# mLSTM heads: row statistics spread by two products with ones instead of small products and diagonals

## The chip, the cores and the metric

The kernel runs on one core of a Trainium2 chip. Its time is the device time of one execution, in microseconds (us); three executions were timed. One further execution was recorded by the profiler, and all rows of the trace come from that one. The engines are PE (TensorE, products; PEld is its weight load), DVE (VectorE), ACT (ScalarE), POOL (GpSimd) and SP (SyncE, which here only issues transfers).

## The reference

The network has two layers on 512 rows of width 1024. The first layer's mixer joins four heads of an mLSTM (192 channels each) and four heads of attention over a memory of 256 rows; an output projection and a gated convolutional MLP follow, then a second layer with banded attention. The part that the change touches is the end of an mLSTM head:

```python
den = jnp.sum(s, axis=-1) + inter * jnp.einsum('bhtd,bhd->bht', qq, n_st)
h = num / jnp.maximum(jnp.abs(den), jnp.exp(-m_t))[..., None]
...
hm = hm * lax.rsqrt(jnp.mean(hm * hm, axis=-1, keepdims=True) + EPS)
hm = hm.reshape(bsz, seq, A_WIDTH) * a_head_g[a].astype(jnp.float32)
mix_out = (hm * jax.nn.sigmoid(o.astype(jnp.float32))).astype(x.dtype)
```

The division by the denominator and the normalisation behind it can be taken together: num times the inverse root of mean(num²) + EPS * max(den², exp(-2 m)). Both kernels do it in this form. `m` is the running stabiliser of a row, and the term with it is called the floor here.

## The kernel before

Activations lie with channels on the 128 partitions and the 512 rows along the free axis. A product in full precision is three products of rounded halves (`mm3`, L166 to L168): high by high, high by low, low by high. The halves come from `split`: a cast on ACT (L122) gives the high half, a subtraction on DVE (L123) the low one. Weights arrive in a raw buffer `wr` by SP's queue and are split in the same way into `wh` and `wl`, of which there are three each; other pools are `u` (57 tiles of 128x512), `t` (8), `bias` (4), and the PSUM banks `mm` (3, in rows `pmm`), `sc` (3, `psc`) and `tr` (2, `ptr`).

`gate_rows` computes the gates once, ahead of the heads. Four rows of 512 (one a head) hold the gates' cumulative sums (`br`), `ar` and the stabiliser (`mr`). The mask exponents go to DRAM (`rowd`) and come back spread over all partitions; `ar` and `mr` are turned to columns by eight 4x4 transposes (L1056, L1057), and ACT makes `floor2` = exp(-2 m) from the second.

`mlstm_head(h)` is a generator. It makes four tiles of weighted scores (L1136: exponential of the mask row; L1142: times the scores, then a split into `pt`), and multiplies them with the values into two `tr` banks: one holds 128 channels, the other 64 channels and, on the other 64 partitions, the denominator 64 times over. ACT squares both banks (L1171) into `t`; DVE multiplies the numerators with the output gate `og` (L1173), which frees the banks. Then, per head:

- eight small products (L1180, L1181; 128x2 out) with the table `mcf` sum the squares of each row over the channels and pick its denominator, with rows now on partitions;
- DVE forms max(den², floor) * EPS + mean (L1185 to L1187, 128x4 each), its inverse root by an integer guess and three Newton steps (`rsqrt`, L214 to L220), and two diagonal tiles of it (`diagonal`, L122, L123 in small, then L229);
- two products of ones with these diagonals (`spread`, L242) bring the factor to all partitions, where it multiplies `og` in place (L1194); each result is split into a pair of tiles in `mixes`, the out-projection's operands.

While a head runs, `weave` advances a second generator, the fill, by so many steps for each yield of the head: projections (`project`, one step is one `mm3`) during heads 0 to 2, pieces of the output projection (`outp.part`) during head 3. The memory attention runs between heads 1 and 2 and between heads 2 and 3. In the profile head 0 ends at about 132 us, head 1 at 163, head 2 at 218, head 3 at 256; its `mixes` are the last operands that the out-projection needs. Where a step needs a tile of these, the code writes out the yields; the order on each engine is then fixed by a scheduler at build time, from the program's dependences, except for operations inside `pin`, which keep their place in program order. Each engine works through its own list in order.

Of the kernel before, what the change touches and what calls it, by code (L numbers as in the profile page):

```python
# [16 lines left out]
P = 128  # L17
# [34 lines left out]
def trunk(  # L52
# [34 lines left out]
    def ps(tag):  # L87
        count[0] += 1
        return psum.tile([P, S], F32, tag=tag, name=f"p{tag}{count[0]}", bufs=pbufs[tag])

    def small(n=4):
        return sb("s", [P, 32])[:, :n]
# [15 lines left out]
    mcf = cpool.tile([P, 3, 2], F32, name="mcf")  # L108
    V.memset(mcf, 0.0)
    V.memset(mcf[:, 0, 0:1], 1.0)  # L110
    V.memset(mcf[:HD, 1, 0:1], 1.0)
    V.memset(mcf[HD:, 1, 1:2], 1.0 / HD)
    V.memset(mcf[:HD, 2, 1:2], 1.0 / HD)
    V.memset(mcf[HD:, 2, 0:1], 1.0)


# [121 lines left out]
    def spread(dgs, tag):  # L238

        o = ps(tag)  # L240
        for i, dg in enumerate(dgs):
            nc.tensor.matmul(o, onesr, dg, start=i == 0, stop=i == 1)  # L242
        return o
# [76 lines left out]
    G.dma_start(gateb, bass.AP(tensor=a_gate_b.tensor, offset=a_gate_b.offset, ap=[[0, P], [1, 2 * AH]]))  # L320
# [39 lines left out]
    def keep(l, i, os_):  # L360
        t = sb("u", [P, S])
        for c, o in enumerate(os_):
            V.tensor_copy(t[:, c * MEM : (c + 1) * MEM], o)
        G.dma_start(spill[l][:, i * S : (i + 1) * S], t)
# [113 lines left out]
    keep(1, 1, vo)  # L478

# [508 lines left out]
    floor2 = cpool.tile([P, TT, AH], F32, name="floor2")  # L988
    RO = [0, 512, 896, 1152, 1280]

    rowd = dram.tile([TT, AH, S], F32, name="rowd")

    def gate_rows():
# [58 lines left out]
        V.tensor_scalar(mr, mr, -40.0, None, op0=ALU.max)  # L1052
        yield
        tp = ps("tr")
        for T in range(TT):
            nc.tensor.transpose(tp[:, T * AH : (T + 1) * AH], ar[:, T * P : (T + 1) * P], ident[:AH, :AH])  # L1056
            nc.tensor.transpose(tp[:, 16 + T * AH : 16 + (T + 1) * AH], mr[:, T * P : (T + 1) * P], ident[:AH, :AH])  # L1057
        pin(V.tensor_copy(acol, tp[:, :16].rearrange("p (t h) -> p t h", t=TT)))
        A.activation(floor2, tp[:, 16:32].rearrange("p (t h) -> p t h", t=TT), AF.Exp, scale=-2.0)
# [53 lines left out]

    def masked(h, s):

        r = exps[h, s]
        pin(
            G.affine_select(
                out=r[:, :P], in_=r[:, :P], pattern=[[1, P]], base=0, channel_multiplier=-1,
                compare_op=ALU.is_ge, fill=NEG,  # L1120
            )
        )

    def mlstm_head(h):
# [3 lines left out]
        rs = slice(HD, P) if odd else slice(0, HD)  # L1128
# [33 lines left out]
        yield from weighted_scores(3)  # L1162
        for s in range(TT if h < AH - 1 else 0):
            exponents(h + 1, s)
# [9 lines left out]
        yield  # L1174
        for s in range(TT if h < AH - 1 else 0):
            masked(h + 1, s)
        st = ps("sc")
        for T in range(TT):
            sl = slice(T * P, (T + 1) * P)
            nc.tensor.matmul(st[:, 2 * T : 2 * T + 2], sqs[0][:, sl], mcf[:, 0, :], start=True, stop=False)  # L1180
            nc.tensor.matmul(st[:, 2 * T : 2 * T + 2], sqs[1][:, sl], mcf[:, 1 + odd, :], start=False, stop=True)  # L1181
            yield 0.581
        st = st[:, : 2 * TT].rearrange("p (t c) -> p t c", c=2)
        z, fc = small(), small()
        V.tensor_tensor(out=z, in0=st[:, :, 1], in1=floor2[:, :, h], op=ALU.max)  # L1185
        V.tensor_scalar(z, z, EPS, 1e-35, op0=ALU.mult, op1=ALU.max)
        V.scalar_tensor_tensor(z, st[:, :, 0], 1.0 / DH, z, op0=ALU.mult, op1=ALU.add)  # L1187
        rsqrt(fc, z)
        dg = diagonal(fc)
        yield 2.673  # L1190
        fb = spread(dg, "sc")
        yield
# [315 lines left out]
```

## Time and profile before

| | us |
|---|---|
| median of 3 runs | 1209.37 |
| lowest and highest | 1208.14, 1210.49 |
| the profiled execution | 1208.28 |
| its span, first to last instruction | 1206.5 |
| granted clock of PE, mean | 0.999 |

A row of the timeline gives the start, the duration, the engine, the line, the operation, output and inputs, the size and how many such rows stand together; brackets give how long the engine had been idle and whose work ended that. Durations of products are modelled and overlap; the distance between two starts is what a product takes. A row of the waits view gives the engine and line that waited, whom for, and the total, the count and the longest.

### The profile page before, as it was taken

Reading aid. Unit: us, or ns where it says so; the run is one execution under the profiler, and the core shown is the slowest. Engines: PE = TensorE matmul, PEld = TensorE weight load, DVE = VectorE, ACT = ScalarE, POOL = GpSimd, SP = SyncE. Lnnn points to the kernel's source line nnn. Section 1 sums busy time; section 2 is a strip of 40 time slices with the busy share of each in tenths; the row PEclk is TensorE's granted clock in tenths of the full one; section 3 lists DMA queues with packets and bytes.
Section 4 is the critical chain, followed back from the end, with each engine's and each line's share of the span. In section 5 each row is a group of like instructions: output and inputs, shape, how many; then the busy total and the mean of one; then the engine's idle time right before and its main releaser. Section 6 shows DMA issues by size and latency. Waiting matters only on the chain.

```text
span 1206.5 us, 18758 instructions
## 1 busy us (share of the span) xinstructions
PE 1191.2 (99%) x7031; PEld 1055.1 (87%) x7031; DVE 938.8 (78%) x1719; ACT 711.9 (59%) x1253; POOL 139.5 (12%) x229
## 2 busy tenths in 40 slices
PE   8999999999999999999999999999999999999997
PEld 8898888888889999999888888888889999999986
DVE  6877688887978777777698888997896777777755
ACT  4547577654655555555565667775565555555545
POOL 0211101011011111111021000101101010111100
PEclk9999999999999999999999999999999999999999
DMA  8646413347565766665564313244845456666551
GB/s 277 200 112 144 91 54 79 109 147 193 123 151 141 161 159 147 153 145 130 148 193 129 93 53 101 68 132 153 194 101 135 114 131 140 141 140 135 121 156 70
DMA packets 206284, 161.79 MB, mean 134 GB/s; under 512 B 8328, under 2 KB 185966, under 8 KB 206194
## 3 DMA queue, kind: packets, MB, share of 16 engines
q1 hardware_dynamic: 184338, 120.78, 34.2%
q0 software_dynamic: 21856, 39.82, 17.7%
q8 instruction: 55, 0.90, 0.3%
q14 instruction: 35, 0.29, 0.1%
HBM read 132.04 MB, written 32.46 MB: 136 GB/s over the span
## 4 chain that ended last, share of the span: by engine, by line
PE 94%; ACT 3%; DVE 2%; DMA 0%; issue 0%; SPq 0%; DVEq 0%; ACTq 0%
PE pmm L166 18%; PE pmm L168 18%; PE pmm L167 18%; PE ptr L166 6%; PE ptr L167 6%; PE ptr L168 6%; PE psc L168 5%; PE psc L167 5%; PE psc L166 5%; PE psc L505 2%; PE ptr L1335 1%; ACT wh L122 1%; PE ptr L1356 1%; PE ptr L1357 1%; DMA u<-in_mem_dram 0%; PE ptr L574 0%
## 5 line engine op out<-in xcount | busy, mean ns | idle before, releaser
L166 PE MATMUL pmm<-u,wh 128*128 128x512 f32 (+1 forms) x968 | 336.6, 348 | 0.1
L168 PE MATMUL pmm<-u,wl 128*128 128x512 f32 (+1 forms) x968 | 333.5, 345 | 0.0
L167 PE MATMUL pmm<-u,wh 128*128 128x512 f32 (+1 forms) x968 | 333.2, 344 | 0.1
L123 DVE TENSOR_TENSOR wl<-wr,wh 128x1024 fp32r<-128x1024 f32 (+4 forms) x168 | 194.5, 1159 | 94.0 <-ACT wh L122 93.4
L122 ACT CAST wh<-wr 128x1024 fp32r<-128x1024 f32 (+4 forms) x168 | 167.7, 1000 | 96.1 <-PE pmm L167 42.1
L168 PEld LDWEIGHTS pmm<-u,wl 128*128 128x128 f32 x968 | 183.6, 190 | 21.1
L167 PEld LDWEIGHTS pmm<-u,wh 128*128 128x128 f32 x968 | 183.9, 190 | 18.4 <-DVE u L123 0.8
L166 PEld LDWEIGHTS pmm<-u,wh 128*128 128x128 f32 x968 | 183.7, 190 | 18.0 <-ACT u L122 0.5
L166 PE MATMUL ptr<-u,wh 128*128 128x512 f32 x272 | 106.7, 392 | 0.0
L167 PE MATMUL ptr<-u,wh 128*128 128x512 f32 x272 | 106.5, 392 | 0.0
L168 PE MATMUL ptr<-u,wl 128*128 128x512 f32 x272 | 105.8, 389 | 0.0
L736 POOL DMA_DIRECT2D xspill<-t x64 | 55.9, 873 | 411.6 <-ACT t L735 411.6
L166 PE MATMUL pmm<-u,u 128*128 128x256 f32 x296 | 84.5, 285 | 2.5 <-ACT t L812 2.5
L168 PE MATMUL pmm<-u,u 128*128 128x256 f32 x296 | 83.9, 284 | 0.2 <-DVE u L123 0.2
L167 PE MATMUL pmm<-u,u 128*128 128x256 f32 x296 | 83.8, 283 | 0.0
L123 DVE TENSOR_TENSOR u<-pt,u 128x512 fp32r<-128x512 f32 x102 | 69.9, 688 | 9.7 <-ACT u L122 7.1
L166 PE MATMUL psc<-u,wh 128*128 128x256 f32 (+1 forms) x232 | 76.1, 328 | 0.0
L735 ACT COPY t<-ptr 128x512 f32<-128x512 f32 x64 | 37.5, 585 | 65.4 <-PE ptr L168 65.4
L167 PE MATMUL psc<-u,wh 128*128 128x256 f32 (+1 forms) x232 | 75.9, 327 | 0.0
L123 DVE TENSOR_TENSOR u<-t,u 128x512 fp32r<-128x512 f32 x78 | 53.4, 689 | 22.0 <-ACT u L122 21.3
L122 ACT CAST u<-pt 128x512 fp32r<-128x512 f32 x102 | 63.0, 617 | 11.5 <-DVE pt L847 11.3
L909 ACT ACTIVATE t<-t 128x512 f32<-128x512 f32 x34 | 21.6, 634 | 80.3 <-DVE t L645 80.3
(282 smaller groups left out, 2562.5 us busy)
## 6 DMA issues: line engine op xcount, KB each, us to landing
wr<-in_ffn_w_up_dram SPq DMA_DIRECT2D x54, 512.0 KB, 4.9
wr<-in_ffn_w_down_dram SPq DMA_DIRECT2D x38, 512.0 KB, 3.8
pt<-in_ffn_w_up_dram SPq DMA_DIRECT2D x34, 512.0 KB, 6.7
xspill<-t POOLq DMA_DIRECT2D x64, 256.0 KB, 4.8
wr<-in_a_w_in_dram SPq DMA_DIRECT2D x20, 512.0 KB, 4.0
xspill<-u POOLq DMA_DIRECT2D x32, 256.0 KB, 2.9
u<-xspill SPq DMA_DIRECT2D x32, 256.0 KB, 5.2
wr<-in_w_kv_dram SPq DMA_DIRECT2D x12, 512.0 KB, 4.2
```

Source lines behind the costliest of these rows:

```text
L122: high = A.copy(hi, src) if on_act else V.tensor_copy(hi, src)
L123: low = V.tensor_tensor(out=lo, in0=src, in1=f(hi), op=ALU.subtract)
L166: nc.tensor.matmul(o, lh, rh, start=first, stop=False, skip_group_check=more)
L167: nc.tensor.matmul(o, lh, rl, start=False, stop=False, skip_group_check=more)
L168: nc.tensor.matmul(o, ll, rh, start=False, stop=last, skip_group_check=more)
L505: nc.tensor.matmul(o, a, b, start=first and i == 0, stop=i == 1)
L735: A.copy(t, o)
L736: G.dma_start(xspill[j], t, accum_op=ALU.add)
L909: A.activation(self.acc, self.acc, AF.Silu)
L1335: nc.tensor.transpose(tp[:, b * P : (b + 1) * P], es[T, h][:, b * P : (b + 1) * P], ident)
L1356: nc.tensor.matmul(o2[:, s * P :], w, hi_at(pts[h], s, s, TT - s), start=s == 0, stop=False)
L1357: nc.tensor.matmul(o2[:, s * P :], w, lo_at(pts[h], s, s, TT - s), start=False, stop=s == TT - 1)
```

## The change

It sums squares and floor on all partitions at once, and computes the inverse root there:

- the table `mcf` and its six memsets, the four transposes of `mr` and `floor2` go;
- `gate_rows` makes the floor as a row: exponential on ACT, times EPS * DH / HD with a lower limit on DVE, stored to DRAM (`floord`) from POOL's queue;
- `den_floor(h)` fetches a head's row, spread over 128 partitions, into a `bias` buffer; its place on POOL's queue is behind the fourth weighted scores and ahead of the next head's four mask rows;
- behind the squares, DVE takes the larger of the scaled den² and the floor on the 64 denominator rows (L1177), adds the two tiles (L1178), and the sum is split;
- two products with ones (L1186) sum over the partitions, the result standing on all of them; ACT takes the inverse root from the bank (L1188, with a table load of its own), DVE does one Newton step on the full tile (L1189 to L1191) and multiplies `og` as before (L1194, now from `t` and not from the bank);
- the yields of a head keep about the same sum, in two pieces instead of six;
- the transfer of the gate biases (4 KB, used first in the value projection's L976) moves from the start to behind the memory keys and values, and two transfers are pinned.

```diff
--- before.py
+++ after.py
@@ -105,15 +105,6 @@
         out=maskf, in_=maskf, pattern=[[1, P]], base=0, channel_multiplier=-1,
         compare_op=ALU.is_ge, fill=NEG,
     )
-    mcf = cpool.tile([P, 3, 2], F32, name="mcf")
-    V.memset(mcf, 0.0)
-    V.memset(mcf[:, 0, 0:1], 1.0)
-    V.memset(mcf[:HD, 1, 0:1], 1.0)
-    V.memset(mcf[HD:, 1, 1:2], 1.0 / HD)
-    V.memset(mcf[:HD, 2, 1:2], 1.0 / HD)
-    V.memset(mcf[HD:, 2, 0:1], 1.0)
-
-
     HEADS = (slice(0, HD), slice(HD, P))
 
     pin = tc.keep_in_program_order
@@ -317,7 +308,6 @@
                 c += k
 
     gateb = cpool.tile([P, 2 * AH], F32, name="gateb")
-    G.dma_start(gateb, bass.AP(tensor=a_gate_b.tensor, offset=a_gate_b.offset, ap=[[0, P], [1, 2 * AH]]))
 
 
 
@@ -361,7 +351,7 @@
         t = sb("u", [P, S])
         for c, o in enumerate(os_):
             V.tensor_copy(t[:, c * MEM : (c + 1) * MEM], o)
-        G.dma_start(spill[l][:, i * S : (i + 1) * S], t)
+        pin(G.dma_start(spill[l][:, i * S : (i + 1) * S], t))
 
     def two_banks(*tags):
         return [ps(tag)[:, :MEM] for tag in tags]
@@ -476,6 +466,7 @@
             x_low(j - 1)
         value_products(vo, *vws1[1], 4)
     keep(1, 1, vo)
+    pin(G.dma_start(gateb, bass.AP(tensor=a_gate_b.tensor, offset=a_gate_b.offset, ap=[[0, P], [1, 2 * AH]])))
 
 
 
@@ -985,10 +976,10 @@
     e, u, c, r = (cpool.tile([P, TT, AH], F32, name=f"gate{i}") for i in range(4))
     tot = cpool.tile([AH, 16], F32, name="tot")
     acol = cpool.tile([P, TT, AH], F32, name="acol")
-    floor2 = cpool.tile([P, TT, AH], F32, name="floor2")
     RO = [0, 512, 896, 1152, 1280]
 
     rowd = dram.tile([TT, AH, S], F32, name="rowd")
+    floord = dram.tile([AH, S], F32, name="floord")
 
     def gate_rows():
 
@@ -1050,13 +1041,14 @@
             yield
         pin(V.tensor_tensor(out=mr, in0=mr, in1=br, op=ALU.add))
         V.tensor_scalar(mr, mr, -40.0, None, op0=ALU.max)
+        A.activation(mr, mr, AF.Exp, scale=-2.0)
+        V.tensor_scalar(mr, mr, EPS * DH / HD, 1e-26 * DH / HD, op0=ALU.mult, op1=ALU.max)
+        pin(G.dma_start(floord, mr))
         yield
         tp = ps("tr")
         for T in range(TT):
             nc.tensor.transpose(tp[:, T * AH : (T + 1) * AH], ar[:, T * P : (T + 1) * P], ident[:AH, :AH])
-            nc.tensor.transpose(tp[:, 16 + T * AH : 16 + (T + 1) * AH], mr[:, T * P : (T + 1) * P], ident[:AH, :AH])
         pin(V.tensor_copy(acol, tp[:, :16].rearrange("p (t h) -> p t h", t=TT)))
-        A.activation(floor2, tp[:, 16:32].rearrange("p (t h) -> p t h", t=TT), AF.Exp, scale=-2.0)
 
     mixes = [None] * KT
 
@@ -1111,6 +1103,14 @@
         pin(G.dma_start(r[:, :n], src))
         exps[h, s] = r
 
+    floors = {}
+
+    def den_floor(h):
+
+        floors[h] = sb("bias", [P, S])
+        src = bass.AP(tensor=floord.tensor, offset=floord.offset + h * S, ap=[[0, P], [1, S]])
+        pin(G.dma_start(floors[h], src))
+
     def masked(h, s):
 
         r = exps[h, s]
@@ -1125,7 +1125,7 @@
         hp, odd = divmod(h, 2)
         sh = 3 * hp + 1
         full = 3 * hp + 2 * odd
-        rs = slice(HD, P) if odd else slice(0, HD)
+        rs, ds = HEADS[odd], HEADS[1 - odd]
         pt = sb("pt", [P, 5 * S], F32R)
 
         def weighted_scores(s):
@@ -1160,6 +1160,7 @@
         yield from weighted_scores(2)
         yield from products(0)
         yield from weighted_scores(3)
+        den_floor(h)
         for s in range(TT if h < AH - 1 else 0):
             exponents(h + 1, s)
         yield from products(1)
@@ -1172,24 +1173,23 @@
             sqs.append(sq)
             V.tensor_tensor(out=og[j][r, :], in0=o[r, :], in1=og[j][r, :], op=ALU.mult)
         yield
+        sq, den = sqs
+        V.scalar_tensor_tensor(den[ds, :], den[ds, :], EPS * DH / HD, floors.pop(h)[ds, :], op0=ALU.mult, op1=ALU.max)
+        V.tensor_add(sq, sq, den)
+        hi, lo = sb("t", [P, S], F32R), sb("t", [P, S], F32R)
+        split(hi, lo, sq)
         for s in range(TT if h < AH - 1 else 0):
             masked(h + 1, s)
-        st = ps("sc")
-        for T in range(TT):
-            sl = slice(T * P, (T + 1) * P)
-            nc.tensor.matmul(st[:, 2 * T : 2 * T + 2], sqs[0][:, sl], mcf[:, 0, :], start=True, stop=False)
-            nc.tensor.matmul(st[:, 2 * T : 2 * T + 2], sqs[1][:, sl], mcf[:, 1 + odd, :], start=False, stop=True)
-            yield 0.581
-        st = st[:, : 2 * TT].rearrange("p (t c) -> p t c", c=2)
-        z, fc = small(), small()
-        V.tensor_tensor(out=z, in0=st[:, :, 1], in1=floor2[:, :, h], op=ALU.max)
-        V.tensor_scalar(z, z, EPS, 1e-35, op0=ALU.mult, op1=ALU.max)
-        V.scalar_tensor_tensor(z, st[:, :, 0], 1.0 / DH, z, op0=ALU.mult, op1=ALU.add)
-        rsqrt(fc, z)
-        dg = diagonal(fc)
-        yield 2.673
-        fb = spread(dg, "sc")
-        yield
+        yield 2.6
+        o = ps("sc")
+        for i, part in enumerate((hi, lo)):
+            nc.tensor.matmul(o, onesr, part, start=i == 0, stop=i == 1)
+        fb, t = sb("t", [P, S]), sb("t", [P, S])
+        A.activation(fb, o, AF.Abs_reciprocal_sqrt, scale=1.0 / DH)
+        V.tensor_mul(t, fb, fb)
+        V.scalar_tensor_tensor(t, t, -0.5 / DH, o, op0=ALU.mult, op1=ALU.mult)
+        V.scalar_tensor_tensor(fb, t, 1.5, fb, op0=ALU.add, op1=ALU.mult)
+        yield 3.4
         for j, r in ((full, slice(0, P)), (sh, rs)):
             V.tensor_tensor(out=og[j][r, :], in0=fb[r, :], in1=og[j][r, :], op=ALU.mult)
             if mixes[j] is None:
```

The lines of the changed kernel move: L122 and L123 are L113 and L114, L166 to L168 are L157 to L159, L1071 is L1063, L1171 is L1172, L1173 is L1174.

First, DVE in head 0, from the gating of the numerators on. Before, where t266 is the fill's convolution (L1071), wl306 a weight's low half and s274 the small statistics:

```order
L1173 TENSOR_TENSOR u223_1210<-ptr249_1346,u223_1210 128x512
L1173 TENSOR_TENSOR u228_1244<-ptr250_1347,u228_1244 64x512
L123 TENSOR_TENSOR wl306_1629<-wr304_1626,wh305_1628 128x1024
L1071 SCALAR_TENSOR_TENSOR t266_1438<-pmm257_1370,cols0_527,t266_1438 128x511
L1071 SCALAR_TENSOR_TENSOR t266_1438<-pmm257_1370,cols0_527,t266_1438 128x510
L1185 TENSOR_TENSOR s274_1491<-psc273_1473,floor2_584 128x4
L1071 SCALAR_TENSOR_TENSOR t266_1438<-pmm257_1370,cols0_527,t266_1438 128x509
L1186 TENSOR_SCALAR s274_1491<-s274_1491 128x4
```

After, where t265 and t266 are the squares, bias260 the floor, t267 the convolution, wl303 the weight's low half and t275 the sum's low half:

```order
L1174 TENSOR_TENSOR u223_1201<-ptr249_1337,u223_1201 128x512
L1174 TENSOR_TENSOR u228_1235<-ptr250_1338,u228_1235 64x512
L1177 SCALAR_TENSOR_TENSOR t266_1428<-t266_1428,bias260_1385 64x512
L114 TENSOR_TENSOR wl303_1600<-wr301_1597,wh302_1599 128x1024
L1063 SCALAR_TENSOR_TENSOR t267_1431<-pmm257_1361,cols0_519,t267_1431 128x511
L1178 TENSOR_TENSOR t265_1425<-t265_1425,t266_1428 128x512
L1063 SCALAR_TENSOR_TENSOR t267_1431<-pmm257_1361,cols0_519,t267_1431 128x510
L114 TENSOR_TENSOR t275_1457<-t265_1425,t274_1456 128x512
L1063 SCALAR_TENSOR_TENSOR t267_1431<-pmm257_1361,cols0_519,t267_1431 128x509
L1189 TENSOR_TENSOR t278_1485<-t277_1484 128x512
```

The weight's low half and two taps of the convolution stand between the new operations of the head, which have the full width.

Second, ACT at the start of head 3, around the last copies of the memory attention (t487 before, t478 after). Before, L1136 are the exponents of the first three score tiles, pt493 the weighted scores, u488 the high half of the memory attention's output and t494 the first product of scores and exponents:

```order
L524 COPY t487_2518<-ptr484_2504 64x512
L1136 ACTIVATE t494_2538<-bias413_2190,acol_583 128x512
L524 COPY t487_2518<-ptr485_2512 64x512
L1136 ACTIVATE t496_2552<-bias414_2192,acol_583 128x384
L122 CAST pt493_2537<-t494_2538 128x512
L1136 ACTIVATE t498_2569<-bias415_2194,acol_583 128x256
L122 CAST u488_2523<-t486_2517 128x512
```

After, with pt484, u479 and t485 in these places, and wh509 a weight of the out-projection:

```order
L113 CAST wh509_2605<-wr508_2600 128x1024
L515 COPY t478_2449<-ptr475_2435 64x512
L515 COPY t478_2449<-ptr476_2443 64x512
L1136 ACTIVATE t485_2469<-bias408_2143,acol_576 128x512
L1136 ACTIVATE t487_2483<-bias409_2145,acol_576 128x384
L1136 ACTIVATE t489_2500<-bias410_2147,acol_576 128x256
L113 CAST u479_2454<-t477_2448 128x512
L113 CAST pt484_2468<-t485_2469 128x512
```

The first cast of weighted scores stood behind two exponents and ahead of u488; now it stands behind three exponents and behind u479.

Third, ACT at the end of head 3. Before, t511 is the square of the second bank, wh532, wh535 and wh553 are weights of the out-projection, and u526 and u442 the high halves of the head's two results:

```order
L1171 ACTIVATE t511_2653<-ptr501_2587 128x512
L122 CAST wh532_2761<-wr531_2758 128x768
L122 CAST wh535_2786<-wr534_2783 128x512
L122 CAST u526_2723<-u434_2318 128x512
L122 CAST u442_2346<-u390_2071 64x512
L122 CAST wh553_2848<-wr552_2846 128x1024
```

After, with t503 the square, t504 the sum's high half, t512 the inverse root, wh520, wh523 and wh541 the weights, u514 and u433 the results:

```order
L1172 ACTIVATE t503_2586<-ptr492_2518 128x512
L113 CAST wh520_2672<-wr519_2669 128x768
L113 CAST t504_2594<-t502_2583 128x512
L1188 ACT_TABLE_LOAD
L1188 ACTIVATE t512_2618<-psc511_2615 128x512
L113 CAST wh523_2697<-wr522_2694 128x512
L113 CAST wh541_2759<-wr540_2757 128x1024
L113 CAST u514_2634<-u426_2252 128x512
L113 CAST u433_2277<-u384_2022 64x512
```

The third weight's cast, which stood behind both results, now stands ahead of them. On PE, the first products that read these results come as two products with u442 (high half of the result) ahead of the first with its low half before, and as five with u433 after.

## The prediction

> **What bounds the kernel now.** I read the page's first lines, then its chain of waits.
>
> ```profile
> span 1206.5 us, 18758 instructions
> PE 1191.2 (99%) x7031; PEld 1055.1 (87%) x7031; DVE 938.8 (78%) x1719; ACT 711.9 (59%) x1253; POOL 139.5 (12%) x229
> PE 94%; ACT 3%; DVE 2%; DMA 0%; issue 0%; SPq 0%; DVEq 0%; ACTq 0%
> ```
>
> PE is busy for all but 15 us of the span and holds 94% of the chain that ends last. So an edit is worth what it takes off PE's row of products, less whatever makes PE wait. The windows view shows the two stretches of the heads that I come back to; its columns are length, busy time with count for PE, PEld, DVE, ACT and POOL, granted clock, DMA share, GB/s.
>
> ```profile
> 160.00:175.00 15.00, 15.00 (x76) 12.65 (x75) 11.56 (x19) 11.52 (x20) 0.00 (x0) 1.00 0.26 71
> 175.00:190.00 15.00, 15.00 (x75) 12.49 (x74) 13.45 (x27) 14.42 (x28) 0.00 (x0) 1.00 0.14 38
> ```
>
> PE has no gap here, the clock is granted in full, and the transfers are light. VectorE and ScalarE are well filled between 160 and 190 us: what is added there can become late. The median of the three runs, 1209.37, is 1.09 above the profiled execution, which took 1208.28: a span of 1206.5 and 1.78 around it. I sum against the profiled execution and carry the difference to the median; about 0.2% (2.4 us) is what a measurement of this kernel tells from no change.
>
> **What is removed.** Now the removed products, by their own rows and, for head 0, in order of time on PE:
>
> ```profile
> L1180 PE MATMUL psc<-mcf,t x32: 165/251/251, 127.8 to 246.9; 128*128 128x2 f32 x32
> 127.79 0.28 PE L1180 MATMUL psc<-mcf,t 128*128 128x2 f32 x2
> 128.46 0.39 PE L167 MATMUL pmm<-u,wh 128*128 128x512 f32 x1
> 128.69 0.40 PE L168 MATMUL pmm<-u,wl 128*128 128x512 f32 x1
> ...
> 131.65 0.40 PE L166 MATMUL pmm<-u,wh 128*128 128x512 f32 x1
> 92.07 0.22 PE L1056 MATMUL ptr<-ident,t 4*128 4x4 f32 x1
> 92.52 0.20 PE L1057 MATMUL ptr<-ident,t 4*128 4x4 f32 x1
> ```
>
> The modelled durations overlap, so I take distances between starts. A 128x512 product starts 0.23 after the one before. From the first small product (127.79) to the first product behind the last one (131.65) go 3.86 us, in which nine such products stand, 9 x 0.2285 = 2.06. The eight small ones (the profile counts each twice: 32 rows of L1180 for 16 products) therefore cost **1.8 us a head**, 7.2 in four heads. In the gate stage eight 4x4 transposes take 92.07 to 92.52 and a little more, 0.06 each; four go, **0.24**. The ones products are two a head before and after. If nothing waited anywhere, the change would be worth 7.4 us: the best end, 1202.0 by the median.
>
> VectorE loses in each head the chain of small operations and two diagonals, and gets six operations of full width. Head 3's chain:
>
> ```profile
> 243.29 1.09 ACT L1171 ACTIVATE t<-ptr 128x512 f32<-128x512 f32 x2 [1.30 <-PE ptr L168]
> 247.43 0.16 DVE L1185 TENSOR_TENSOR s<-psc,floor 128x4 f32<-128x4 f32 x1 [0.79 <-PE psc L1181]
> 250.49 1.29 DVE L229 TENSOR_TENSOR t<-ident,s 128x512 fp32r<-128x512 f32 x2
> 252.40 0.62 ACT L122 CAST wh<-wr 128x512 fp32r<-128x512 f32 x1 [6.75 <-PE ptr L167]
> 254.64 1.41 DVE L123 TENSOR_TENSOR u<-u,u 128x512 fp32r<-128x512 f32 x2
> 255.35 0.61 PE L166 MATMUL pmm<-u,wh 128*128 128x512 f32 x2
> 255.37 1.05 ACT L122 CAST wh<-wr 128x1024 fp32r<-128x1024 f32 x1 [0.71 <-PE ptr L167]
> 256.10 0.50 PE L167 MATMUL pmm<-u,wh 128*128 128x512 f32 x1
> 256.45 1.23 DVE L123 TENSOR_TENSOR wl<-wr,wh 128x1024 fp32r<-128x1024 f32 x1 [0.40 <-ACT wh L122]
> ```
>
> Removed are 3.06 us of small operations (247.43 to 250.49) and 1.29 of L229; added are L1177, L1178, the low subtraction and L1189 to L1191 at 0.65 to 0.7 each, like one of the two in row 254.64: about 4.1. VectorE is even. ScalarE gets a cast and an inverse root, about 0.6 each, and a table load. No row shows an inverse root or a Newton step reading a bank; I take them at the cost of a 128x512 operation between SBUF and a bank, one of the two in 243.29 (0.54) and 0.7, with 0.3 more as upper end for each.
>
> **New waits.** Before, the small products read the squares directly. Now the ones products need floor, sum and split first; engines work in order, so what stands between counts. Head 0:
>
> ```profile
> 126.14 1.28 DVE L1173 TENSOR_TENSOR u<-ptr,u 128x512 f32<-128x512 f32 x2 [1.66 <-ACT t L1171]
> 127.56 1.23 DVE L123 TENSOR_TENSOR wl<-wr,wh 128x1024 fp32r<-128x1024 f32 x1
> 128.71 1.53 DVE L1071 SCALAR_TENSOR_TENSOR t<-pmm,cols,t 128x511 f32<-128x511 f32 x2
> 151.23 1.42 DVE L1173 TENSOR_TENSOR u<-ptr,u 128x512 f32<-128x512 f32 x2 [2.68 <-ACT t L1171]
> 208.65 0.68 DVE L1173 TENSOR_TENSOR u<-ptr,u 64x512 f32<-64x512 f32 x1
> ```
>
> VectorE is free of L1173 at 127.42; then by the changed order L1177 (0.68), the weight low half (1.23, less 0.05 overlap), one tap (0.75) and the sum (0.69): 130.7; the high cast 0.62: 131.35. PE has fourteen products between the old place and the first ones product: 127.79 + 14 x 0.2285 = 130.99. It waits 0.4, and head 0 keeps **1.4**. In head 1 nothing stands ahead of the high cast: 152.65 + 0.68 + 0.69 + 0.62 = 154.64, against the first small product at 152.16 plus nine products, 154.2: wait 0.45; I take off another 0.2 for the first memory attention, whose ScalarE stretch starts later with a table load more: **1.15**. In head 2 the third tap (0.64) stands between: 208.65 + 0.68 + 0.64 + 0.68 + 0.69 + 0.62 = 212.0, against its first small product plus seventeen, 207.75 + 3.88 = 211.6: wait 0.4.
>
> ```profile
> 152.16 0.28 PE L1180 MATMUL psc<-mcf,t 128*128 128x2 f32 x2
> 207.75 0.28 PE L1180 MATMUL psc<-mcf,t 128*128 128x2 f32 x2
> 236.06 0.60 ACT L122 CAST pt<-t 128x512 fp32r<-128x512 f32 x1
> 236.57 0.51 ACT L1136 ACTIVATE t<-bias,acol 128x256 f32<-128x256 f32 x1
> 236.98 0.60 ACT L122 CAST u<-t 128x512 fp32r<-128x512 f32 x1
> ```
>
> Between head 2 and head 3 ScalarE's order changes: the third exponent (0.51) and the memory-attention cast (0.60) now stand ahead of the first cast of weighted scores, on which PE's next product with pt waits. That is 1.05 later, once the overlap is taken off. Of head 2's 1.8 there remain 1.8 - 0.4 - 1.05 = **0.35**.
>
> Head 3 has no cover behind it, since the out-projection's last products need its tiles. Before, PE reached them at 255.35, did two high products, waited briefly for the low half and began the third at 256.10, the seventh four products and that start's 0.1 later, at 257.1. After, PE reaches them 1.8 - 0.5 earlier, at 254.05. But the order puts the weight cast wh541 ahead of u514 and u433. Its buffer comes free only with PE's last product before, at about 254.0, so the casts end at 254.05 + 1.05 + 0.6 + 0.6 = 256.3. PE waits 2.3, does five high products (1.14) and waits 0.25 again for the last low half (weight low 1.23, two subtractions 1.41, from 255.1: 257.75). The sixth then starts at 257.75 and the seventh, like 256.10 to its next, 0.34 behind it at 258.1: head 3 **loses 1.0**.
>
> **Table loads.** Five more loads, one a head and one in the gate stage:
>
> ```profile
> 169.27 1.28 ACT L1072 ACT_TABLE_LOAD   x1
> 170.57 0.63 ACT L1072 ACTIVATE t<-t 128x512 f32<-128x512 f32 x1
> ```
>
> A load takes 1.28, and the activation behind it starts 0.02 after its end. A head's load stands ahead of its inverse root, which waits for the ones products; in head 3 ScalarE sat idle for 6.75 us there (row 252.40). The load costs nothing while such idle time covers it, 1.28 if not. The Trainium skill, "ScalarE: Activation LUTs", section "What ACT_TABLE_LOAD costs", gives 1283 ns for the load and 1380 ns more for a drain at every switch of set. The load agrees with the trace's 1.28 us; a drain doesn't show behind it, where 169.27 to 170.57 leaves no room. By the page, heads 0 and 1 would put 2.8 us more on ScalarE ahead of the stretch at 160 us, and rival C would weigh more; I go by the rows.
>
> **Edits at nothing, and their cover.** The gate stage's exponential, table load and store lie behind products of the projections; ScalarE is 11.5 of 18 us busy there.
>
> ```profile
> 82.00:100.00 18.00, 18.00 (x85) 14.74 (x84) 13.91 (x23) 11.50 (x17) 5.84 (x13) 1.00 0.59 125
> 97.49 0.29 POOL L1118 TENSOR_SCALAR_AFFINE_SELECT bias<-bias 128x128 f32<-128x128 f32 x1 [1.39 <-DMA bias<-rowd]
> 106.88 0.55 POOL L1111 DMA_DIRECT2D bias<-rowd  x1 [9.10 <-ACT t L1136]
> bias<-rowd POOLq DMA_DIRECT2D x4, 256.0 KB, 3.9
> 7.76 0.66 PE L429 MATMUL psc<-ident,u 128*128 128x128 f32 x4 [1.77 <-DMA u<-in_mem_dram]
> ```
>
> The first masks, last at 97.49, come some 4 us later on GpSimd and are used after 104. The floor's broadcast stands on GpSimd's queue ahead of the next head's four rows; in head 0 that is at 106.9, some twenty us before L1177 reads it; in head 3 its buffer is free once the first exponent has read it, by 236, ten us ahead. Its buffer delays the next head's fourth row, which has as long. Uncovered, it would cost its landing, 3.9 like a row of the same size. Moving the gate biases' 4 KB from the start may let the memory tile that PE waits 1.77 for land sooner: 0 to 0.3, and I take 0; at their new place behind 41 us they have ten us before use. The six memsets lie before the first transfers land.
>
> **Sum.** 0.24 + 1.4 + 1.15 + 0.35 - 1.0 = 2.1 us less: 1206.2 by the profiled execution, **1207.3** by the median. Ends: each wait may be 0.3 off, five of them 1.5 together: 1205.8 to 1208.8.
>
> **Rivals.** **B: the waits in heads 0 to 2 don't come,** because ScalarE and VectorE run ahead where I placed them in a row. Then 0.24 + 3 x 1.8 - 1.0 = 4.6: 1204.7, down to 1202.0 if head 3's cast isn't late either. For it: modelled rows overlap, and the waits are 0.4 each. Against: the casts and subtractions are serial in the code.
>
> **C: ScalarE becomes the bound between 160 and 190.** It is busy 25.9 of 30 us there, and head 1's tail arrives with 0.6 + 0.6 + 1.28 more. It would swallow what heads 0 and 1 gained, 2.55: 0.4 slower, 1209.8. For it: the 14.42 of 15. Against: 160 to 175 has 3.5 idle.
>
> **D, the slower side: the weight low half stands in front of the sum.** In heads 0, 1 and 3 VectorE does such a half between the new operations, and it can itself wait for its high cast:
>
> ```profile
> DVE wl L123 <- ACT wh L122: 109.5, 122, 4.2
> ```
>
> The waits view gives sum, count and longest: 0.9 on average, 4.2 at worst. If two heads met the longest, 8.4 - 2.1 = 6.3 slower, 1215.7. From 2.1 us of such waits together, or 0.7 a head, the gain is gone; from 4.5 it is slower by more than a measurement needs. For it: 109.5 us of such waits in the kernel. Against: in head 0 the half at 127.56 follows its neighbours without one.
>
> **E: the small products were hidden,** PE having been in wait for VectorE beside them. But 1.8 us go between 127.79 and 131.65 with no releaser named in any row of PE there, so I give it no chance.
>
> **How the numbers follow.** Forecast 0.53, B 0.19, C 0.17, D 0.11. The forecast's range 1205.8 to 1208.8 has the 0.2% line at 1207.0 near its middle: 0.26 faster, 0.27 same. With B, faster is 0.45; with C, same is 0.44; slower is D, 0.11. The range leaves out most of D and the lower part of B: 1204.0 to 1211.0.
>
> **What would show it.** Right: no rows of the small products; PE waits of about 0.4 at the ones products in three heads, near 1.05 at the first product with pt in head 3, near 2.3 ahead of the out-projection's last tiles, released by the cast u433. Wrong: a clean PE at the ones products (B), PE gaps between 160 and 190 released by ScalarE (C), or by a weight low half (D).

## The result, and the profile after

| | before | after |
|---|---|---|
| median of 11 runs, us | 1209.46 | 1206.7 |
| lowest to highest | 1208.14 to 1210.49 | 1205.07 to 1208.52 |
| ratio, 95% interval | | 0.9981 (0.9973 to 0.999) |
| span of the profiled execution | 1206.5 | 1204.9 |

The changed kernel is 0.19% faster, 2.3 us by the ratio; the forecast was 2.1. The total was near, but the terms that make it up are others than I wrote. First the page's lines on the span and the busy times, after:

```profile
span 1204.9 us, 18596 instructions
PE 1185.9 (98%) x6963; PEld 1048.4 (87%) x6963; DVE 940.3 (78%) x1666; ACT 723.1 (60%) x1266; POOL 145.1 (12%) x234
```

PE does 5.3 us less, the span is 1.6 us shorter: most of what PE no longer does has become waiting. To see where, I use three marks that every kernel has: the first transpose of the input x (L384 before, L374 after), the first product of the norm's statistics behind the mixer (L266 before, L257 after), and the end of the span. Their rows, before and after (minimum, median and longest duration in ns, first and last start):

```profile
L384 PE MATMUL psc<-ident,pt x16: 272/272/273, 27.1 to 30.1; 128*128 128x128 f32 x16
L266 PE MATMUL psc<-ones,rb x24: 164/250/250, 282.3 to 849.4; 128*128 128x1 f32 x24
```

```profile
L374 PE MATMUL psc<-ident,pt x16: 272/273/273, 25.4 to 28.4; 128*128 128x128 f32 x16
L257 PE MATMUL psc<-ones,rb x24: 164/250/250, 279.1 to 847.0; 128*128 128x1 f32 x24
```

Already at 25 us, before anything of the heads, 1.7 us are gained. From there to the statistics it takes 253.7 and not 255.2, and from the statistics to the end 925.8 and not 924.2. So: **1.7 us at the start, 1.5 in the gates and heads, and 1.6 lost again behind the mixer.**

The start. The memory tile that PE waited 1.77 us for, and the same row after:

```profile
5.58 0.60 PE L419 MATMUL psc<-ident,u 128*128 128x128 f32 x4
```

It has no bracket and starts at 5.58 in place of 7.76. The view of transfers in the first 12 us, in 40 slices, before:

```profile
GB/s 0 0 0 0 0 0 123 229 358 304 345 372 161 158 125 117 25 9 90 200 215 263 362 365 386 382 386 369 362 352 362 335 355 352 338 365 335 352 355 335
```

and after:

```profile
GB/s 0 0 0 0 0 0 27 256 369 318 331 379 348 365 198 191 290 317 328 372 338 328 372 321 331 219 287 314 345 341 355 338 331 362 345 379 386 369 365 369
```

Before, the rate falls to 25 and 9 GB/s in slices 17 and 18, at 5 us; after, it stays above 190 once it is up. The 4 KB of gate biases were fetched there: GpSimd issues them at 1.66 us, and they land 5.8 us later, at about 7.5, just ahead of the product that waited.

```profile
1.66 0.72 POOL L320 DMA_DIRECT2D gateb<-in_a_gate_b_dram  x1
gateb<-in_a_gate_b_dram POOLq DMA_DIRECT2D x1, 4.0 KB, 5.8
```

The heads. Before, PE has no row in the view of waits between 100 and 235 us. After, it has these (total, count, longest):

```profile
PE psc L1186 <- ACT t L113: 1.0, 3, 0.4
PE psc L157 <- DVE t L1142: 0.5, 1, 0.5
PE ptr L157 <- ACT pt L113: 0.2, 1, 0.2
```

And the end of head 3 in order of time:

```profile
241.87 0.50 PE L1186 MATMUL psc<-t,onesr 128*128 128x512 f32 x1 [0.44 <-ACT t L113]
243.38 1.28 ACT L1188 ACT_TABLE_LOAD   x1 [1.56 <-PE psc L1186]
244.67 0.60 ACT L1188 ACTIVATE t<-psc 128x512 f32<-128x512 f32 x1
247.96 1.41 DVE L1194 TENSOR_TENSOR u<-t,u 128x512 f32<-128x512 f32 x2
248.63 1.04 ACT L113 CAST wh<-wr 128x1024 fp32r<-128x1024 f32 x1 [2.14 <-PE ptr L158]
249.58 1.25 ACT L113 CAST u<-u 128x512 fp32r<-128x512 f32 x2
250.89 1.61 PE L157 MATMUL pmm<-u,wh 128*128 128x512 f32 x3 [2.11 <-ACT u L113]
253.15 0.63 PE L158 MATMUL pmm<-u,wh 128*128 128x512 f32 x1
253.57 0.63 PE L159 MATMUL pmm<-u,wl 128*128 128x512 f32 x1
```

PE waits 2.11 us for the cast of the head's result, behind the next weight's cast, as the prediction has it. Two things are not in it. The table load starts only when the low ones product has ended (its bracket names PE), so its 1.28 us lengthen the way to the head's result. Yet the wait doesn't end on that way here: VectorE's multiplications (L1194) are done at 249.37, the first after about half of their 1.41, and the results' casts follow the weight's cast, which one of PE's last products ahead of the wait released (L158). And behind the wait products start 0.42 us apart, not 0.23. The windows view over these 3.5 us (the third column from the end is the granted clock):

```profile
250.90:254.40 3.50, 3.50 (x8) 2.75 (x9) 1.32 (x3) 0.00 (x0) 0.00 (x0) 0.51 0.50 149
```

Behind the mixer, PE waits for a weight transfer for which it did not wait before:

```profile
294.81 0.50 PE L159 MATMUL psc<-u,pt 128*128 128x512 f32 x1 [0.70 <-DMA pt<-in_ffn_w_up_dram]
```

### The profile page after: what moved, and what is told of

It is laid out like the page before. It is cut to its first block, busy times and chain, and to the rows that moved or that the text cites. A ratio compares the mean times of both kernels' runs of the same rounds, so it can differ in the third digit from the quotient of the medians.

```text
span 1204.9 us, 18596 instructions
## 1 busy us (share of the span) xinstructions
PE 1185.9 (98%) x6963; PEld 1048.4 (87%) x6963; DVE 940.3 (78%) x1666; ACT 723.1 (60%) x1266; POOL 145.1 (12%) x234
## 4 chain that ended last, share of the span: by engine, by line
PE 80%; issue 12%; DVE 2%; DMA 2%; ACT 2%; POOL 1%; POOLq 0%; SPq 0%; ACTq 0%; DVEq 0%
PE pmm L157 15%; PE pmm L159 15%; PE pmm L158 15%; PE ptr L158 5%; PE ptr L157 5%; PE ptr L159 5%; PE psc L159 5%; PE psc L157 4%; PE psc L158 4%; PE psc L496 2%; DMA pt<-in_ffn_w_up_dram 2%; PE ptr L1335 1%; POOL xspill L610 1%; ACT wh L113 0%; PE ptr L1356 0%
## 5 line engine op out<-in xcount | busy, mean ns | idle before, releaser
L157 PE MATMUL pmm<-u,wh 128*128 128x512 f32 (+1 forms) x968 | 336.3, 348 | 2.2 <-ACT u L113 2.1
L158 PE MATMUL pmm<-u,wh 128*128 128x512 f32 (+1 forms) x968 | 333.6, 345 | 0.0
L159 PE MATMUL pmm<-u,wl 128*128 128x512 f32 (+1 forms) x968 | 333.4, 345 | 0.0
L114 DVE TENSOR_TENSOR wl<-wr,wh 128x1024 fp32r<-128x1024 f32 (+4 forms) x168 | 194.5, 1158 | 96.5 <-ACT wh L113 95.5
L113 ACT CAST wh<-wr 128x1024 fp32r<-128x1024 f32 (+4 forms) x168 | 167.9, 1000 | 93.9 <-PE pmm L158 44.5
L157 PEld LDWEIGHTS pmm<-u,wh 128*128 128x128 f32 x968 | 183.9, 190 | 21.2 <-ACT u L113 3.1
L159 PEld LDWEIGHTS pmm<-u,wl 128*128 128x128 f32 x968 | 183.9, 190 | 21.1
L158 PEld LDWEIGHTS pmm<-u,wh 128*128 128x128 f32 x968 | 184.1, 190 | 18.2 <-DVE u L114 0.2
L157 PE MATMUL ptr<-u,wh 128*128 128x512 f32 x272 | 106.8, 394 | 0.0
L158 PE MATMUL ptr<-u,wh 128*128 128x512 f32 x272 | 106.5, 392 | 0.0
L159 PE MATMUL ptr<-u,wl 128*128 128x512 f32 x272 | 105.8, 389 | 0.0
L157 PE MATMUL pmm<-u,u 128*128 128x256 f32 x296 | 84.5, 285 | 2.8 <-ACT t L803 2.8
L159 PE MATMUL pmm<-u,u 128*128 128x256 f32 x296 | 84.0, 284 | 0.4 <-DVE u L114 0.4
L158 PE MATMUL pmm<-u,u 128*128 128x256 f32 x296 | 83.8, 283 | 0.0
L114 DVE TENSOR_TENSOR u<-pt,u 128x512 fp32r<-128x512 f32 x102 | 69.8, 687 | 9.7 <-ACT u L113 7.1
L157 PE MATMUL psc<-u,wh 128*128 128x256 f32 (+1 forms) x232 | 76.1, 328 | 0.0
L158 PE MATMUL psc<-u,wh 128*128 128x256 f32 (+1 forms) x232 | 75.9, 327 | 0.0
L114 DVE TENSOR_TENSOR u<-t,u 128x512 fp32r<-128x512 f32 x78 | 53.3, 688 | 22.6 <-ACT u L113 22.2
L113 ACT CAST u<-pt 128x512 fp32r<-128x512 f32 x102 | 63.0, 618 | 11.4 <-DVE pt L838 11.2
```

Of the source, the lines that this page charges most:

```text
L113: high = A.copy(hi, src) if on_act else V.tensor_copy(hi, src)
L114: low = V.tensor_tensor(out=lo, in0=src, in1=f(hi), op=ALU.subtract)
L157: nc.tensor.matmul(o, lh, rh, start=first, stop=False, skip_group_check=more)
L158: nc.tensor.matmul(o, lh, rl, start=False, stop=False, skip_group_check=more)
L159: nc.tensor.matmul(o, ll, rh, start=False, stop=last, skip_group_check=more)
```

## The experiments

Theories: that the fetch of the gate biases alone makes the start faster; that the heads give what the sum said; that the table load, the Newton step or the order of casts makes head 3's end late; that the clock falls for the wait. Where an expectation speaks of the transposes of the memory keys, the mark is the first transpose of x (its input `pt` holds x).

### again: the changed kernel, unaltered

> The changed kernel once more, nothing altered. If its marks in time are properties of the program, they return: the second memory tile's transposes start at about 5.6 us (7.8 before), the first products of the norm's statistics at 279.1 us (282.3 before), PE waits 2.1 us ahead of the out-projection's last tiles, and the granted clock in the 3.5 us behind that wait is near 0.51. The rival: the fall of the clock, or the wait of 0.7 us for a weight transfer at 294.8 us, belongs to that one execution and is not there again; then the marks behind it lie 1 to 2 us earlier.

Measured: ratio 0.9987 (0.9979 to 0.9996). The marks return but for one: the statistics start at 278.0. The wait of 2.11 us is there, and behind it:

```profile
251.00:254.50 3.50, 3.48 (x14) 2.58 (x15) 1.35 (x3) 0.00 (x0) 0.00 (x0) 1.00 0.50 150
```

Fourteen products in place of eight: the clock held this time. The wait for the channel mixer's transfer is there again (0.7). So the wait belongs to the program, the fall of the clock to the one execution; it costs 1.1 us at the statistics.

### bias_moved_only: the kernel before, with the fetch moved

```diff
-    G.dma_start(gateb, bass.AP(tensor=a_gate_b.tensor, ...))
...
-        G.dma_start(spill[l][:, i * S : (i + 1) * S], t)
+        pin(G.dma_start(spill[l][:, i * S : (i + 1) * S], t))
...
     keep(1, 1, vo)
+    pin(G.dma_start(gateb, bass.AP(tensor=a_gate_b.tensor, ...)))
```

> The kernel before, with one part of the change alone: the gate biases' 4 KB fetched behind the memory keys and values, and the two pins. Theory: their transfer at the start held back the second memory tile, so PE's wait of 1.77 us at 7.76 us goes, the transposes of the memory keys start at 25.4 us and not 27.1, the norm's statistics at 280.5 and not 282.3; the whole kernel is 1.2 to 1.8 us faster. Rival: the start got faster for the memsets that the change removes on VectorE; then nothing moves here: 27.1, 282.3, the same time.

Measured: ratio 0.9984 (0.9975 to 0.9993), as much as the whole change. First transpose of x at 25.7, statistics at 280.8, no wait for the memory tile; the memsets are still there, so they were not it. The span of its profiled execution is only 0.5 us shorter than that of before; the profiled execution of before, 1208.28, is among the shorter of its kind, whose median is 1209.46. PE waits 0.73 us for the channel mixer's transfer there too.

### bias_at_start: the changed kernel, with the fetch at the start

```diff
     gateb = cpool.tile([P, 2 * AH], F32, name="gateb")
+    G.dma_start(gateb, bass.AP(tensor=a_gate_b.tensor, ...))
...
-    pin(G.dma_start(gateb, bass.AP(tensor=a_gate_b.tensor, ...)))
```

> The changed kernel with the gate biases fetched at the start again, on GpSimd's queue as before. Theory: PE waits 1.8 us for the second memory tile again, the memory keys' transposes start at 27.1 us, the norm's statistics at 280.9; 1.2 to 1.8 us slower than the changed kernel, that is 1 us faster than the kernel before at most. Rival (the memsets): no wait, 25.4 us, and the time of the changed kernel.

Measured: ratio 0.9997 (0.9988 to 1.0006). The wait is back (1.46), x's first transpose at 28.1, 1.0 later than expected. The wait itself isn't longer than in the kernel before; the products of 128x256 behind it stand 0.21 us apart until 10.4 us, where they stood 0.12 apart in the profile of before:

```profile
9.14 0.41 PE L157 MATMUL pmm<-u,u 128*128 128x256 f32 x1
9.35 0.41 PE L158 MATMUL pmm<-u,u 128*128 128x256 f32 x1
```

The column of the granted clock has 1.00 for that stretch, so it doesn't say why. From x's first transpose to the statistics it takes 252.3 us: the heads' gain is there in full at this mark, 2.9 us. But at the end nothing is left that could be measured.

### bias_at_start_sync: the same, issued by SyncE

```diff
+    nc.sync.dma_start(gateb, bass.AP(tensor=a_gate_b.tensor, ...))
```

> The changed kernel with the gate biases fetched at the start, in the same 128 pieces of 32 bytes, but issued by SyncE ahead of its loads and not by GpSimd. If the pieces themselves hold the memory tiles back, PE waits for the second tile as in the kernel before, 1 to 2 us. If it is GpSimd's queue that does it, the loads are only issued later by the one issue more, about 0.5 us: transposes of the memory keys at 25.4 to 25.9 us.

Measured: ratio 0.9986 (0.9978 to 0.9995); x's first transpose at 27.1. PE doesn't wait for the second tile, but 0.84 us for the first one, and the rate of transfers is 41 to 61 GB/s in slices 8 to 10 of the first 12 us, where the changed kernel has 256 to 369. Neither expectation fits alone: the small fetch costs on this queue too, ahead of the first tile and not the second. The gap can't be put down to GpSimd's queue. The ratio, though, is that of the repeat (0.9987): the time doesn't show the 1.7 us at x's first transpose.

### before_again: the kernel before, unaltered

> The kernel before once more, nothing altered. Its profile had no wait of PE for the channel mixer's transfer near 297 us, and the four others so far had 0.4 to 0.7 us there. If that is chance in the landing of a transfer that has no slack, it may show 0 to 0.9 us here; if the kernel before escapes it by its order, it shows none again. The norm's statistics start at 282.3 us within 0.2.

One execution: 1209.18 us, x's first transpose at 28.3, statistics at 283.3, 1.0 later than expected, 924.1 from there to the end. The wait for the memory tile was 2.15, 0.4 longer than in the first profile, and behind it the granted clock fell to half, from 8 to 11 us:

```profile
8.00:11.00 3.00, 3.00 (x16) 3.00 (x16) 1.29 (x2) 1.10 (x2) 0.00 (x0) 0.50 1.09 362
```

So the kernel before lost at its start the wait alone in one profile, and the wait with products at half speed behind it in the other. No wait for the channel mixer's transfer, as in the first profile.

### load_ahead_head3: the table loaded before the ones products end

```diff
         split(hi, lo, sq)
+        if h == AH - 1:
+            A.activation(small(1), f(hi)[:, :1], AF.Abs_reciprocal_sqrt)
```

> The changed kernel with one more small activation in head 3: an inverse root of one column of the sum's high half, right behind that half's cast, so that the table is loaded while PE still works on the ones products. Theory: the load of 1.28 us stands behind the low product's semaphore and lengthens the end of head 3 by as much; with it gone, and with the results' casts then ordered ahead of the next weight's, PE's wait of 2.1 us falls to 0.1 to 0.4 and the one for the low halves to about 0.5, the granted clock stays at 1.00, and the norm's statistics start 1.5 to 2 us earlier than in the repeat of the changed kernel: 276.0 to 276.5 us. Rival: the Newton step's three operations on VectorE are what makes the end late; then the wait stays above 1 us.

Measured: 1203.52 us, ratio **0.9958** (0.9945 to 0.997). ScalarE at the end of head 3:

```profile
243.36 1.28 ACT L1182 ACT_TABLE_LOAD   x1
244.65 0.20 ACT L1182 ACTIVATE s<-t 128x1 f32<-128x1 f32 x1
244.87 0.60 ACT L1190 ACTIVATE t<-psc 128x512 f32<-128x512 f32 x1
```

The load has no bracket: it starts behind the high half's cast. PE's wait of 2.11 us is gone altogether, with the Newton step in place, so the step alone doesn't make the end late. This edit also put the results' casts ahead of the next weight's, and no run parts the two. An estimate from the rows of the changed kernel says how they share it. In its order the wait ends on the weight's cast, so an earlier load alone would leave it near 2.1. In the other order, with the load where it was, casts right behind the multiplications' end at 249.37 would end near 250.0 and not at 250.83, and 1.2 to 1.3 of the wait would be left. By that it takes both. The statistics start at 276.9 and not 276.0 to 276.5, for a reason that lies elsewhere: the clock fell in this execution behind a wait that all these kernels have at 42 us.

```profile
42.08 0.81 PE L157 MATMUL pmm<-wh,u 128*128 128x392 f32 x3 [1.45 <-ACT wh L113]
43.20:46.80 3.60, 3.60 (x12) 3.60 (x13) 2.77 (x5) 1.99 (x3) 3.60 (x11) 0.53 0.97 294
```

### busy_wait_head3: products that nobody reads in the wait

```diff
+            if h == AH - 1 and j == full:
+                w = ps("sc")
+                for _ in range(8):
+                    nc.tensor.matmul(w[:, :P], ones, og[j][:, :P], start=True, stop=True)
```

> The changed kernel with eight products on PE whose result nobody reads, 128x128, placed in the wait at the end of head 3 (they need the head's first result, which is there when the wait begins). Theory of the clock: PE's idle time there lets the granted clock fall to half for 3.5 us in some executions (in one of four profiles so far). With the wait filled the clock is 1.00 behind it and the norm's statistics start at 278.0 us, as in the repeats where the clock held; a full execution gains nothing over those and up to 1.1 us over the others. Rival: the products delay the out-projection's own by their length, and the statistics start at 279 us or later.

Measured: ratio 0.998 (0.9971 to 0.9988). The filling products run from 248.85 on for 2.05 us, PE's own begin at 251.05, the clock is 1.00, the statistics start at 278.0. They cost nothing at this mark. PE waited 1.01 us for the second memory tile in this profile, with the biases' fetch moved away, and still x's first transpose stood at 25.5: that wait by itself doesn't make the start late. That the filling products save anything is not shown: the clock also holds in executions without them.

### longer_wait_head3: three Newton steps in head 3

```diff
+        for _ in range(3 if h == AH - 1 else 1):
...
```

> The changed kernel with the Newton step done three times instead of once in head 3 alone: PE's wait ahead of the out-projection's last tiles grows from 2.1 us to 6.0 to 6.5. Theory: the clock falls once PE has been idle for part of some stretch that doesn't begin with the wait; a wait of 2 us meets it now and then, one of 6 us always. Then the granted clock is near 0.5 for some 3.5 us behind the wait in any execution, and the norm's statistics start at 283.8 to 284.5 us: 278.0 plus 4.2 for the longer wait, 0.5 for the low halves and 1.6 for the clock; three to six us slower than the changed kernel. Rival: the fall in the changed kernel's profile was a disturbance that has nothing to do with the wait; then the clock stays at 1.00 and the statistics start at 282.2 to 282.8 us.

Measured: ratio 1.0036 (1.0024 to 1.0048), statistics at 284.1. The wait and the clock:

```profile
255.49 0.79 PE L157 MATMUL pmm<-u,wh 128*128 128x512 f32 x1 [6.69 <-ACT u L113]
250.00:253.00 3.00, 0.00 (x0) 0.00 (x0) 2.93 (x5) 0.00 (x0) 0.00 (x0) 0.91 0.34 103
253.00:255.00 2.00, 0.00 (x0) 0.00 (x0) 1.90 (x4) 0.80 (x2) 0.00 (x0) 0.50 0.70 202
255.60:258.60 3.00, 3.00 (x7) 2.01 (x8) 0.63 (x1) 0.00 (x0) 0.00 (x0) 0.50 0.00 0
259.20:262.00 2.80, 2.80 (x14) 2.29 (x13) 1.07 (x2) 0.78 (x2) 0.51 (x1) 0.98 0.00 0
```

The wait is a little longer than the 6.0 to 6.5 expected, and so is the time: some 6 us more than the changed kernel by the ratios. The clock falls while PE stands idle and comes back some 3.7 us after it works again. It is the idle time that brings the fall; this profile can't say that it comes in every execution, as expected, since it is one.

### no_newton: the inverse root without its Newton step

```diff
-        V.tensor_mul(t, fb, fb)
-        V.scalar_tensor_tensor(t, t, -0.5 / DH, o, op0=ALU.mult, op1=ALU.mult)
-        V.scalar_tensor_tensor(fb, t, 1.5, fb, op0=ALU.add, op1=ALU.mult)
```

> The changed kernel without the Newton step behind the inverse root, in all four heads: three operations of 128x512 less on VectorE, 2.1 us a head, the table load where it was. If VectorE's chain sets the end of head 3, PE's wait there goes altogether and the statistics start 1.7 to 2.3 us earlier than in the repeat of the changed kernel (278.0): 275.7 to 276.3 us. If the table load alone mattered, the wait shrinks by no more than the order of casts gives, 0.8 us, to about 1.3. In heads 0 to 2 nothing changes on PE (0.3 us together), since the fill covers what stands behind the ones products.

Measured: 1201.97 us, ratio **0.995** (0.9936 to 0.9964). It leaves out the step, so its factor has the table's precision alone. The wait at the end of head 3 is gone with the table load where it was, so the load alone doesn't make the end late either. Here, too, the results' casts stand ahead of the next weight's. Gone are also the two between heads 2 and 3 (0.5 and 0.2; the scheduler's order differs there). The statistics start at 274.5, 3.5 earlier than in the repeat, where 1.7 to 2.3 were expected: 2.1 for the wait, those 0.7, and 0.7 that no wait in the view accounts for.

### load_ahead_more_fill and no_newton_more_fill: more products ahead of the first ones product

```diff
-        yield 2.6
+        yield 3.6
...
-        yield 3.4
+        yield 2.4
```

> The kernel with the table loaded ahead in head 3, and the two yields of a head at 3.6 and 2.4 instead of 2.6 and 3.4, so that one product more stands ahead of the first ones product in head 0 and three more in head 1. Theory: PE's waits of 0.2 to 0.4 us there are the time by which the sum's high half is late; they go in head 1 (0.4) and fall to 0.1 in head 0, and head 1's second ones product then has less in between, 0.1 us of wait at most. 0.4 to 0.6 us faster than without, too little for a verdict: 1202.9 to 1203.2 by the median; the waits decide. Rival: the waits move to the second ones product, 0.3 us each.

> Without the Newton step in all heads, and with the two yields at 3.6 and 2.4. The same waits as in the run without the step fall by 0.4 to 0.6 us in heads 0 and 1: 1201.4 to 1201.7 by the median, 6.5 to 7 us below the kernel before. Rival as there: the waits move to the second ones product and the time stays at 1202.0.

Measured: ratios 0.9956 (0.9944 to 0.9969) and 0.9951 (0.9937 to 0.9964), against 0.9958 and 0.995 without. In both profiles head 0's wait of 0.2 is gone, and head 1's of 0.4 has moved to the second ones product (0.35, for DVE's low half): in head 0 the expectation, in head 1 the rival. The time doesn't show it. The clock held at 42 us in both, and with the table loaded ahead the statistics start at 275.8.

## Why the prediction came out near, point by point

The three marks in all kernels (us; the first transpose of x, the norm's statistics, and the two stretches between; from the trace):

| kernel | x | statistics | x to statistics | statistics to end |
|---|---|---|---|---|
| before | 27.1 | 282.3 | 255.2 | 924.2 |
| before_again | 28.3 | 283.3 | 255.0 | 924.1 |
| after | 25.4 | 279.1 | 253.7 | 925.8 |
| again | 25.4 | 278.0 | 252.6 | 926.3 |
| bias_moved_only | 25.7 | 280.8 | 255.1 | 925.2 |
| bias_at_start | 28.1 | 280.4 | 252.3 | 925.9 |
| bias_at_start_sync | 27.1 | 279.4 | 252.3 | 926.2 |
| load_ahead_head3 | 25.6 | 276.9 | 251.3 | 926.1 |
| busy_wait_head3 | 25.5 | 278.0 | 252.5 | 926.6 |
| longer_wait_head3 | 25.6 | 284.1 | 258.5 | 927.3 |
| no_newton | 25.4 | 274.5 | 249.1 | 925.5 |
| load_ahead_more_fill | 25.9 | 275.8 | 249.9 | 925.9 |
| no_newton_more_fill | 25.7 | 274.9 | 249.2 | 926.6 |

- **The start, taken at 0 with an upper end of 0.3: wrong, 1.7.** The row of the wait stood in the prediction, but no row stood behind the price of 0 to 0.3. The trace of before has both: the fetch in flight from 1.66 to about 7.5 us, and the rate at 9 GB/s around 5 us. All four profiles with the fetch at the start have x's first transpose at 27.1 to 28.3, all nine without it at 25.4 to 25.9. Alone, the move gives a ratio of 0.9984: as much as the whole.
- **Removed products, 7.44: right.** Without the step, the waits left in gates and heads are the four at the ones products, 1.0 + 0.4. 7.44 - 1.4 = 6.0, and the table has 255.1 - 249.1 = 6.0. That also settles rival E, the hidden products.
- **Waits at the ones products, 0.4, 0.45, 0.4 and 0.5: right,** 0.2, 0.4, 0.4 and 0.44. Rival B's case for heads 0 to 2 didn't come.
- **Between heads 2 and 3, 1.05: 0.65, and most of it elsewhere.** The first product with `pt`, which the prediction names, waits 0.19. Ahead of it the fourth score tile's product waits 0.46 for its bank, released by VectorE's L1142; the prediction has no such wait:

```profile
232.19 0.33 PE L157 MATMUL psc<-u,u 128*128 128x128 f32 x1 [0.46 <-DVE t L1142]
233.05 0.73 PE L157 MATMUL ptr<-pt,u 128*128 128x512 f32 x2 [0.19 <-ACT pt L113]
```

- **The end of head 3, a wait of 2.3: right,** 2.11, and on the way that the prediction names: the weight's cast starts with one of PE's last products, and the results' casts come behind it. What the prediction has otherwise is the table load. It let ScalarE's idle time cover it, but the load stood behind the product, as the activation did. That lengthened the way to the results by 1.28, the price named for this case. In this order of casts it doesn't show in the wait; in the other order it would be about what is left of it, by the estimate above.
- **The low halves behind it, 0.25:** hidden in the slow products of the first profile, in the repeat no more than the view of waits leaves out.
- **Gates and heads in sum, 2.1: measured 2.4 to 2.9** where the clock held (255.0 to 255.2 less 252.3 to 252.6), 1.4 where it fell. The clock was not in the sum at all.
- **Behind the mixer, nothing: wrong, 1.0 to 3.1 us longer** in every kernel but the two profiles of before. PE's waits account for most of it: 0.9 us for the up-projection's transfers in the two channel mixers and 0.3 more than before for ScalarE (L803, 2.8 and not 2.5) are 1.2 of the changed kernel's 1.6; 1.5 and 0.3 are 1.8 of the repeat's 2.1. The first of these transfers has no slack. GpSimd issues it 5.4 us behind the statistics before and 5.5 after, so the issue moved along with PE, but it is 9.3 us in flight before and 10.2 after. Why, stays open: bias_moved_only has 10.2 too, with the heads of before.

So the sum was met because a gain of 1.7 that I had at nothing and a loss of 1.6 that I hadn't seen are of one size. That is luck. Rival C's place, 160 to 190 us, shows no wait of PE for ScalarE, and rival D's wait for a weight's low half doesn't show either.

## What to carry to other kernels

Ask of a small transfer not how many bytes it has but what it holds up: 4 KB spread over 128 partitions cost 1.7 to 2.9 us at x's first transpose beside the first loads, and the same 4 KB at 40 us cost nothing that the marks show. Where a function needs a table of its own and stands at the end of a chain, let a tiny activation whose input is there earlier load it ahead; in head 3 that, together with the order of casts that came with it, took a wait of 2.1 us away and made the kernel 0.42% faster than before, more than twice what the change gave. And read a gain at several marks: what was won by 279 us was partly lost by the end.

## What the hardware showed beside that

The granted clock of TensorE fell to half behind short waits, in some executions: behind 2.11 us at the end of head 3 in one of four profiles (the first, the repeat, bias_at_start and bias_at_start_sync have that wait); behind 2.15 us at the memory tile in before_again; behind 1.45 us at 42 us in load_ahead_head3, one of thirteen profiles with that wait; and within the 6.69 us of longer_wait_head3. Work ran at half speed for about 3.5 us each time; between the first profile and the repeat that made 1.1 us at the statistics. The Trainium skill, "TensorE: Matmul & The Clock Gate", Part 1, says that the gate watches a free-running window of about 3.4 us and that an idle window returns it to half speed, a busy one to full speed. The return after some 3.7 us of work agrees; here gaps of well under one window were enough. A wait of 2 us on PE therefore has a price of its own that a count of products doesn't show, and one that varies from run to run.
